# A fused mixer and feed-forward layer: retention's transposes two ticks sooner in the order, and softmax's scaling ahead of the next exponential

## The chip, the cores and the metric

The kernel runs on one core of a Trainium2 chip. The metric is device time in microseconds (us), the median over executions. The engines are TensorE (PE, with its weight loads PEld), VectorE (DVE), ScalarE (ACT), GpSimd (POOL) and SyncE (SP, here the queue that requests nearly all transfers). Each engine works through its own instructions in the order in which the program gives them.

## The reference, cut to what matters

One layer over 256 tokens of width 1024, all in fp32. The change touches the token mixer's two halves, attention and retention:

```python
proj = h @ w_in                                  # q, k, v of both, a gate rg, gates g_a and g_r
y_a  = moba_attention(mq, mk, mv)                # 8 heads of 64; one block of 256 keys, so plain causal softmax
y_r  = silu(rg) * head_norm(retention(rq, rk, rv))          # 4 heads, values of 256
merged = sigmoid(g_a) * (y_a @ w_proj_moba) + sigmoid(g_r) * (y_r @ w_proj_ret)
y = merged @ w_out
x = layer_norm(ALPHA * x + g1 * y, ...)          # then the feed-forward part and a second norm
```

## The kernel before, in words

All products of activations with weights are made in three matmuls of split operands: every fp32 weight half (128 x 1024) is split into a high part `whi` (an ACT copy with rounding, L1264) and a low part `wlo` (a DVE subtraction, L1278), and the product is high by high, high by low and low by high (`mm3`, L123 to L125). Activations are split in the same way by `split` (ACT L100, then DVE L101). A weight arrives as 1 MB in one of four buffers `raw`, requested on SP's queue (L110) when DVE has finished with the buffer's former content. Between the weight halves DVE also makes the products of the conditioning vector with its matrix (`ada`, L263, with its read of the sum; L989 ends a section); these use `raw` buffers too.

Nothing schedules at run time: the program writes the instructions of all engines in one order. The main loop goes over *steps*, one weight half of 1024 columns each. Three times a step it advances the *side* generators by one tick (`run_sides`): once ahead of the preparation of further weight halves, once behind it and ahead of the step's matmuls, and once behind the matmuls. `mixers` (attention) and `retention` are such generators, and a `yield` is a tick; so a count of empty `yield`s sets where a side's work stands among the weights' work. `put_off(n, fn)` does something n steps later.

Attention: `scores` and `maxima` (DVE L1059) come four and two heads at a time into the tiles `sm`, then for iteration i ACT takes the exponential of head i-1 with its sum (L1082), DVE the reciprocal of that sum (L1090), and ACT scales head i-3 (L1087); groups of heads are then transposed on PE (L1098) and copied back (L1100). `L504` evacuates the products of the rotated queries and keys.

Retention: its values lie in `yr`, the tiles A8a and A8b, one for each half of the tokens. At the end ACT scales them by the norm (L1180), DVE multiplies them with the gate (L1184), PE transposes them in 16 pieces into the four PSUM banks 4 to 7 (L1199), and `split` makes of these the two tiles `yr2` (AYa and AYb).

What follows one another on PE there: the gate products of `winGr` (evacuated by the sigmoid at L537), `wpm` (attention's projection, two groups of 24 matmuls), and `wpr` (retention's projection, two groups of 48, which read `yr2`). The banks of one group of 512 columns are those of the group two before: the first group of `wpr` writes the banks of the first group of `wpm`, which DVE empties by

```python
dve.tensor_tensor(v, bk[t], v, OP.mult)       # L544, in pm_done
```

Of the kernel before, what the change touches and what calls it, by code (L numbers as in the profile page):

```python
# [9 lines left out]
AF = mybir.ActivationFunctionType  # L10
# [3 lines left out]
HM, DM = 8, 64  # L14
# [54 lines left out]
def _body(nc, a, out, pe, act, dve, sp, cst, wts, big, tmp, ps, dram):  # L69
    f = lambda ap: ap.bitcast(F32)  # L70

    def bank(i):
        return ps.tile([128, 512], F32, tag=f"P{i}", name=f"P{i}")
# [10 lines left out]
    def slot(n, shape, dt=F32):  # L84
        if n in pairs:
            assert pairs[n].dtype == dt
            return pairs[n].rearrange("p e (k t) -> p e k t", k=shape[2])
        if n not in place:
            return big.tile(shape, dt, tag=f"A{n}", name=f"A{n}")
        pair, e = place[n]  # L90
        assert pairs[pair].dtype == dt
        v = pairs[pair][:, e, :math.prod(shape[1:])]
        return v.rearrange("p (a b) -> p a b", a=shape[1]) if len(shape) == 3 else v
# [5 lines left out]
    def split(hi, lo, src):  # L99
        act.activation(hi, src, AF.Copy)  # L100
        dve.tensor_tensor(lo, src, f(hi), OP.subtract)  # L101
# [927 lines left out]
    def mixers():  # L1029


        for _ in range(3 * SCORES_AT):
            yield
        v = S["v"]
        S["decay"] = [slot(n, [128, 2, 384]) for n in ("6a", "6b")]
        for i in range(2):
            nc.gpsimd.dma_start(S["decay"][i], a["decay"][i])
        st, pt = {}, {}
        blk = [slice(128 * qb, 128 + 256 * qb) for qb in range(2)]

        def scores(h):


            S["sc"] = [bank(b) for b in (4, 7, 5, 6)]
            x = S["rot"][h // 4]
            for qb, c in enumerate(blk):
                for i in range(2):
                    for e in range(4):
                        s = slice(32 * e, 32 * e + 32)
                        pe.matmul(S["sc"][e][:, c], x[s, i, qb * 128:(qb + 1) * 128], x[s, 2 + i, :128 + 128 * qb],  # L1050
                                  start=i == 0, stop=i == 1)

        def maxima(h):

            for e in range(2):
                sm = S["sms"][:, (h + e) % (TL + 2)]
                mx = tmp.tile([128, 8], F32, name="mx", bufs=TL + 2)
                for qb, c in enumerate(blk):
                    dve.tensor_tensor_reduce(out=sm[:, c], in0=S["sc"][h % 4 + e][:, c],  # L1059
                                             in1=consts["mask"][:, 128 - 128 * qb:],  # L1060
                                             scale=-0.125, scalar=3.0e38, op0=OP.add, op1=OP.min,
                                             accum_out=mx[:, 2 + qb:3 + qb])
                st[h + e] = sm, mx

        def attend(h, p):

            for w in range(2):
                pT = [pt.pop(h + 2 * w + e) for e in range(2)]
                for kb, (o, c) in enumerate(((slice(0, 256), slice(0, 256)), (slice(128, 256), slice(256, 384)))):
                    for e in range(2):  # L1070
                        u = h + 2 * w + e
                        pe.matmul(p[64 * e:64 * e + 64, 256 * w + o.start:256 * w + o.stop],
                                  v[:, kb, 64 * u:64 * u + 64], pT[e][:, c], start=kb == 0, stop=kb == 1)
            return lambda: split(S["yah"][:, h // 2:h // 2 + 2], S["yal"][:, h // 2:h // 2 + 2],
                                 p.rearrange("p (w t) -> p w t", w=2))

        for i in range(HM + 5):
            yield
            if 0 <= i - 1 < HM:
                sm, mx = st[i - 1]  # L1080
                for qb, c in enumerate(blk):
                    act.activation(sm[:, c], sm[:, c], AF.Exp, scale=-1.0, bias=mx[:, 2 + qb:3 + qb],  # L1082
                                   accum_out=mx[:, 4 + qb:5 + qb])
            if 0 <= i - 3 < HM:
                sm, rx = st[i - 3]
                for qb, c in enumerate(blk):
                    act.activation(sm[:, c], sm[:, c], AF.Copy, scale=rx[:, 6 + qb:7 + qb])  # L1087
            yield
            if 0 <= i - 1 < HM:
                dve.reciprocal(mx[:, 6:8], mx[:, 4:6])  # L1090
            if i == HM + 4:
                S["yah"], S["yal"] = [slot(n, [128, 4, 256], F32R) for n in ("5", "15")]
                done = [attend(4 * g, bank(5 + g)) for g in range(2)]
            for h in {6: (0, 1), 9: (2, 3, 4, 5), 11: (6, 7)}.get(i, ()):
                sm, mx = st.pop(h)
                p = bank((4, 7, 4, 7, 5, 6, 4, 7)[h])
                for b in range(3):
                    pe.transpose(p[:, b * 128:(b + 1) * 128], sm[:, b * 128:(b + 1) * 128], ident)  # L1098
                pT = sm if h > 1 else slot(("9a", "9b")[h], [128, 384])
                act.activation(pT, p[:, :384], AF.Copy)  # L1100
                pt[h] = pT
            if i == 0:
                S["sms"] = slot(11, [128, TL + 2, 384])
            if i in (0, 4):
                scores(i)
            if i in (0, 2, 4, 6):
                maxima(i)
            if i == RET_AT:
                sides.append(retention())
            yield  # L1110
        for fn in done:
            fn()

    def retention():
# [13 lines left out]
        for n in range(4):  # L1128
# [8 lines left out]
            if n == 1:  # L1137
                yr = [slot(n, [128, 1024]) for n in ("8a", "8b")]
                for g in range(HR):
                    d_ = ds_.pop(g)  # L1140
                    p = bank(VALUES[g])
                    c = slice(g * 256, (g + 1) * 256)
# [33 lines left out]
        for g in range(HR + 1):  # L1176
# [4 lines left out]
            if g < HR:  # L1181
                c = slice(g * 256, (g + 1) * 256)
# [7 lines left out]
        yrh, yrl = [[t[:, i] for t in S["yr2"]] for i in range(2)]  # L1190
        for _ in range(3):
            yield
        for _ in range(8):
            yield
        ps = [bank(4 + i) for i in range(4)]
        for i, p in enumerate(ps):
# [108 lines left out]
    prep_to(FIRST + 2)  # L1305
    evac_B()
    sides = [mixers()]

    def run_sides():
# [148 lines left out]
```

## Time and profile before

| | |
|---|---|
| median of 3 executions | 424.75 us (423.34 to 424.86) |
| the profiled execution | 423.23 us, its span 421.5 us |
| PE busy | 412.2 us |
| DVE busy | 370.3 us |
| ACT busy | 251.6 us |
| granted TensorE clock | 1.0 |
| read from memory | 104.28 MB, 250 GB/s over the span |

The span runs from the first to the last instruction; the rest of the execution's time, 1.7 us, lies around it. A row of the timeline gives the start in us, the duration in us, the engine and line, the operation, what it writes and reads, and in brackets how long the engine was idle before it and what released it. Instructions of one engine overlap a little, so what one costs in a row of its like is best read from start to start. SP's rows are requests, not transfers.

### The profile page before, as it was taken

The numbers are of one execution on the slowest core, as the hardware profiler recorded it, in microseconds if no ns is written. First come the engines' busy times: TensorE is split into PE (matmuls) and PEld (weight loads), VectorE is DVE, ScalarE is ACT, GpSimd is POOL, SyncE is SP. The second block draws the span as 40 slices with busy tenths as digits, with TensorE's granted clock in tenths as the row PEclk, the third lists the DMA queues.
The fourth block names the chain that finished last, engine by engine and source line by source line (L and its number), as shares of the span: only waits on it lengthen the run. The fifth ranks groups of instructions, "written<-read, shape, count | busy, mean of one in ns | idle before, by whom it ended". The sixth has DMA issues, their size and how long they took to land.

```text
span 421.5 us, 5942 instructions
## 1 busy us (share of the span) xinstructions
PE 412.2 (98%) x2156; PEld 347.0 (82%) x2156; DVE 370.3 (88%) x593; ACT 251.6 (60%) x442; POOL 14.0 (3%) x26
## 2 busy tenths in 40 slices
PE   7999999999999999979999999999999999999995
PEld 4888888888878888868888898888888888888884
DVE  6979798889997689799987889999999998789996
ACT  5666568687994885435553896373554555455700
POOL 0000010000000100000000000100000000003200
PEclk9999999999999999999999999999999999999999
DMA  8998999656574969978882073895867877550002
GB/s 298 405 409 342 412 402 417 253 201 211 198 282 149 341 227 370 332 275 317 338 303 101 0 301 111 306 383 200 303 242 251 308 282 268 192 200 2 0 2 100
DMA packets 18685, 105.73 MB, mean 251 GB/s; under 512 B 2272, under 2 KB 3680, under 8 KB 7904
## 3 DMA queue, kind: packets, MB, share of 16 engines
q1 hardware_dynamic: 17136, 99.84, 62.6%
q0 software_dynamic: 1376, 4.99, 3.3%
q10 hardware_dynamic: 144, 0.52, 0.5%
q8 instruction: 17, 0.28, 0.3%
q14 instruction: 12, 0.10, 0.1%
HBM read 104.28 MB, written 1.06 MB: 250 GB/s over the span
## 4 chain that ended last, share of the span: by engine, by line
PE 79%; DVE 10%; DMA 4%; ACT 4%; issue 2%; DVEq 0%; ACTq 0%
PE P L134 21%; PE P L337 13%; PE P L138 11%; PE P L123 9%; PE P L125 9%; PE P L124 9%; DVE wlo L1278 2%; DVE junk L263 2%; DMA raw<-in_wpr 2%; DMA raw<-in_wpm 2%; ACT AYa L1134 1%; ACT whi L1264 1%; DMA raw<-in_m 1%; PE P L721 1%; PE P L724 1%
## 5 line engine op out<-in xcount | busy, mean ns | idle before, releaser
L1278 DVE TENSOR_TENSOR wlo<-raw,whi 128x1024 fp32r<-128x1024 f32 x118 | 141.8, 1219 | 15.8 <-ACT whi L1264 15.6
L1264 ACT ACTIVATE whi<-raw 128x1024 fp32r<-128x1024 f32 x118 | 121.3, 1054 | 39.0 <-DMA raw<-in_wpr 15.6
L134 PE MATMUL P<-AYa,whi 128*128 128x512 f32 x160 | 46.3, 391 | 0.0
L134 PE MATMUL P<-AYb,whi 128*128 128x512 f32 x160 | 43.0, 390 | 0.0
L337 PE MATMUL P<-whi,AH 128*128 128x512 f32 x160 | 41.6, 390 | 0.5 <-DVE AH L303 0.5
L263 DVE CUSTOM_DVE_ANT_0 junk<-raw,srow 128x1024 bf16<-128x1024 f32 x32 | 39.0, 1217 | 0.0
L123 PE MATMUL P<-whi,AH 128*128 128x512 f32 x96 | 38.0, 396 | 0.0
L125 PE MATMUL P<-whi,AH 128*128 128x512 f32 x96 | 37.4, 390 | 0.0
L124 PE MATMUL P<-wlo,AH 128*128 128x512 f32 x96 | 37.4, 389 | 0.0
L337 PEld LDWEIGHTS P<-whi,AH 128*128 128x128 f32 x160 | 30.0, 188 | 7.5 <-ACT whi L320 1.3
L134 PEld LDWEIGHTS P<-AYb,whi 128*128 128x128 f32 x160 | 30.0, 188 | 6.6
L134 PEld LDWEIGHTS P<-AYa,whi 128*128 128x128 f32 x160 | 28.8, 189 | 4.7
L481 ACT ACTIVATE A<-P 128x256 f32<-128x256 f32 x40 | 15.1, 377 | 29.0 <-PE P L138 17.1
L134 PE MATMUL P<-AH,whi 128*128 128x512 f32 x128 | 31.6, 394 | 0.0
L320 ACT ACTIVATE whi<-raw 128x512 fp32r<-128x512 f32 (+1 forms) x26 | 20.8, 824 | 17.4 <-DMA raw<-in_b 16.2
L323 DVE TENSOR_TENSOR wlo<-raw,whi 128x512 fp32r<-128x512 f32 (+1 forms) x26 | 23.6, 935 | 6.1 <-ACT whi L320 5.6
L134 PEld LDWEIGHTS P<-AH,whi 128*128 128x128 f32 x128 | 23.3, 188 | 5.1 <-issue 0.3
L138 PE MATMUL P<-AYb,wlo 128*128 128x256 f32 x160 | 25.7, 283 | 0.0
L138 PE MATMUL P<-AYa,wlo 128*128 128x256 f32 x160 | 25.6, 283 | 0.0
L138 PEld LDWEIGHTS P<-AYa,wlo 128*128 128x128 f32 x160 | 23.3, 190 | 1.6
L337 PE MATMUL P<-wlo,AH 128*128 128x512 f32 x80 | 23.2, 389 | 0.0
L810 DVE SCALAR_TENSOR_TENSOR A<-A,tables 128x255 f32<-128x255 f32 (+1 forms) x44 | 21.3, 483 | 1.6
(310 smaller groups left out, 760.0 us busy)
## 6 DMA issues: line engine op xcount, KB each, us to landing
raw<-in_ada SPq DMA_DIRECT2D x16, 1024.0 KB, 4.8
raw<-in_wup SPq DMA_DIRECT2D x11, 1024.0 KB, 6.4
raw<-in_wgate SPq DMA_DIRECT2D x11, 1024.0 KB, 6.0
raw<-in_wdown SPq DMA_DIRECT2D x11, 1024.0 KB, 5.0
raw<-in_wrot SPq DMA_DIRECT2D x8, 1024.0 KB, 8.0
raw<-in_m SPq DMA_DIRECT2D x4, 1024.0 KB, 8.3
raw<-in_b SPq DMA_DIRECT2D x4, 1024.0 KB, 7.3
raw<-in_winGr SPq DMA_DIRECT2D x4, 1024.0 KB, 5.4
```

The lines of the kernel that those rows point to most:

```text
L123: pe.matmul(o, lh, rh, start=start, stop=False)
L124: pe.matmul(o, lh, rl, start=False, stop=False)
L125: pe.matmul(o, ll, rh, start=False, stop=stop)
L134: pe.matmul(banks()[half], t[0][:, k * 128:(k + 1) * 128], x2(k), start=k == 0, stop=half > 0 and k == 7)
L138: pe.matmul(banks()[half][:, :256], t[1][:, k * 128:(k + 1) * 128], x2(k)[:, 0], start=False, stop=half == 0 and k == 7)
L263: dve.tensor_tensor_reduce(out=nobody(j if own else None), in0=raw, in1=srow, scale=1.0, scalar=0.0, op0=OP.mult, op1=OP.add, accum_out=mo ...
L320: act.activation(hi[:, o], raw[:, o], AF.Copy)
L323: dve.tensor_tensor(lo[:, o], raw[:, o], f(hi[:, o]), OP.subtract)
L337: pe.matmul(pa[b0 + c // 512 * 2 + t], x[xi][:, j, t * 128:(t + 1) * 128], ws[k][:, c:c + 512], start=first and (xi, k) == (0, 0), stop=la ...
L810: dve.scalar_tensor_tensor(g[:, 2 - n:], x[:, :254 + n], w(n), g[:, 2 - n:], op0=OP.mult, op1=OP.add)
L1264: act.activation(hi, src, AF.Copy)
L1278: dve.tensor_tensor(lo, src, f(hi), OP.subtract)
```

## The change

Two places are written in another order; no instruction is added, removed or made larger.

```diff
         for i in range(HM + 5):
             yield
+            if 0 <= i - 3 < HM:
+                sm, mx = st[i - 3]
+                for qb, c in enumerate(blk):
+                    act.activation(sm[:, c], sm[:, c], AF.Copy, scale=mx[:, 6 + qb:7 + qb])
             if 0 <= i - 1 < HM:
                 sm, mx = st[i - 1]
                 for qb, c in enumerate(blk):
                     act.activation(sm[:, c], sm[:, c], AF.Exp, ...
-            if 0 <= i - 3 < HM:
-                ...
...
-        for _ in range(8):
+        for _ in range(6):
             yield
         ps = [bank(4 + i) for i in range(4)]
```

In `retention` two ticks are taken out ahead of the transposes, so they and their splits are written ahead of the preparation of weight halves in that step and of its matmuls.

On PE the 16 transposes (L1199) stood between the two halves of `wpm`'s first group; they now stand ahead of the whole group, right behind the last matmul of `winGr`. On ACT, around the sigmoids of `winGr` (L537), in the difference of the two orders:

```order
 L537 ACTIVATE A_1569<-P_1583 128x512
-L1264 ACTIVATE whi<-raw 128x1024
-L100 ACTIVATE AYa<-P_1683 128x4x128
-L100 ACTIVATE AYa<-P_1684 128x4x128
-L100 ACTIVATE AYb<-P_1685 128x4x128
-L100 ACTIVATE AYb<-P_1686 128x4x128
-L1264 ACTIVATE whi<-raw 128x1024 x10
+L100 ACTIVATE AYa<-P_1661 128x4x128
+L100 ACTIVATE AYa<-P_1662 128x4x128
+L100 ACTIVATE AYb<-P_1663 128x4x128
+L100 ACTIVATE AYb<-P_1664 128x4x128
+L1264 ACTIVATE whi<-raw 128x1024 x11
```

The four splits have moved past one weight half, the first of the second unit of `wpr`; all that follows on ACT keeps its order.

On DVE, from the end of a section of `ada` (L989) to the emptying of `wpm`'s banks (L544), before:

```order
L989 TENSOR_TENSOR mod<-mod,first 128x8
L1278 TENSOR_TENSOR wlo<-raw,whi 128x1024
L263 ISA junk,mod<-raw,srow 128x1024
L263 ISA mod 128x1
L101 TENSOR_TENSOR AYa<-P_1683,AYa 128x4x128
L101 TENSOR_TENSOR AYa<-P_1684,AYa 128x4x128
L101 TENSOR_TENSOR AYb<-P_1685,AYb 128x4x128
L101 TENSOR_TENSOR AYb<-P_1686,AYb 128x4x128
L1278 TENSOR_TENSOR wlo<-raw,whi 128x1024
L263 ISA junk,mod<-raw,srow 128x1024
L263 ISA mod 128x1
L544 TENSOR_TENSOR A_1414<-P_1669,A_1414 128x512
```

and the same place now:

```order
L989 TENSOR_TENSOR mod<-mod,first 128x8
L101 TENSOR_TENSOR AYa<-P_1661,AYa 128x4x128
L101 TENSOR_TENSOR AYa<-P_1662,AYa 128x4x128
L101 TENSOR_TENSOR AYb<-P_1663,AYb 128x4x128
L101 TENSOR_TENSOR AYb<-P_1664,AYb 128x4x128
L1278 TENSOR_TENSOR wlo<-raw,whi 128x1024
L263 ISA junk,mod<-raw,srow 128x1024
L263 ISA mod 128x1
L1278 TENSOR_TENSOR wlo<-raw,whi 128x1024
L263 ISA junk,mod<-raw,srow 128x1024
L263 ISA mod 128x1
L544 TENSOR_TENSOR A_1414<-P_1697,A_1414 128x512
```

The four low halves of the split have moved past one weight half (the second of the first unit of `wpr`) and one product of `ada`. The first L1278 there is the last reader of a `raw` buffer, so SP's next request of `wpr` waits for it, though SP's own order and POOL's stay as they are.

In the softmax, on ACT, one iteration (exponential L1082 before and L1086 now, scaling L1087 before and L1082 now, for the two blocks of queries; `mx` holds the maxima, sums and reciprocals):

```order
 L1264 ACTIVATE whi<-raw 128x1024 x2
-L1082 ACTIVATE A_838,mx<-A_838,mx 128x128
-L1082 ACTIVATE A_838,mx<-A_838,mx 128x256
-L1087 ACTIVATE A_838<-A_838,mx 128x128
-L1087 ACTIVATE A_838<-A_838,mx 128x256
+L1082 ACTIVATE A_838<-A_838,mx 128x128
+L1082 ACTIVATE A_838<-A_838,mx 128x256
+L1086 ACTIVATE A_838,mx<-A_838,mx 128x128
+L1086 ACTIVATE A_838,mx<-A_838,mx 128x256
 L504 ACTIVATE AR_585<-P_1125 128x256
```

The scaling of head i-3 now stands ahead of the exponential of head i-1 in each iteration. DVE's and PE's orders there are unchanged.

More of the change, by code (lines that the diff above doesn't have):

```diff
@@ L1083, in mixers @@
                                    accum_out=mx[:, 4 + qb:5 + qb])
-            if 0 <= i - 3 < HM:
-                sm, rx = st[i - 3]
-                for qb, c in enumerate(blk):
-                    act.activation(sm[:, c], sm[:, c], AF.Copy, scale=rx[:, 6 + qb:7 + qb])
             yield
```

## The prediction

> **What bounds the kernel now.** I read the page's busy shares first, then who waited for whom on TensorE (PE) and its weight loads (PEld), then the chain that ended last, then the order of time around the two places that the change touches.
>
> ```profile
> PE 412.2 (98%) x2156; PEld 347.0 (82%) x2156; DVE 370.3 (88%) x593; ACT 251.6 (60%) x442; POOL 14.0 (3%) x26
> ```
>
> PE is busy for 412.2 of 421.5 us, so an edit that leaves its work alone can win only what PE idles. The waits (total us, times, longest) say where that is:
>
> ```profile
> PE P L123 <- DVE A L544: 2.5, 1, 2.5
> ...
> PEld P L123 <- issue: 2.9, 1, 2.9
> ...
> PEld P L1098 <- ACT A L1087: 0.7, 2, 0.5
> ```
>
> The largest idle time is one event: the first matmul of `wpr` waits 2.5 us for VectorE's (DVE's) L544. The other is small: the transposes of the softmax rows (L1098) wait twice, 0.7 us in all, for ScalarE's (ACT's) scaling at L1087. The windows (us, then busy time of PE, PEld, DVE, ACT, POOL, then the granted clock, DMA share, GB/s) bound it:
>
> ```profile
> 158.00:184.00 26.00, 23.59 (x113) 19.44 (x111) 22.23 (x35) 13.42 (x22) 0.00 (x0) 1.00 0.83 320
> 186.00:411.00 225.00, 225.00 (x1170) 193.10 (x1169) 205.33 (x317) 121.50 (x188) 10.96 (x16) 1.00 0.58 214
> ```
>
> Between 158 and 184 PE loses 2.4 us; from 186 to 411 it loses nothing, so no transfer or engine is late there, and what PE gains before 186 it keeps unless the sooner start makes something late. The chain shows what the long wait consists of:
>
> ```profile
> 158.07 6.89 DMA raw<-in_wpm
> ...
> 169.61 7.30 DMA raw<-in_wpr
> ...
> 177.96 0.59 ACT AYa L100
> ...
> 182.10 1.22 DVE junk L263
> 183.33 0.61 DVE A L544
> 184.08 0.47 PE P L123
> ```
>
> A transfer of `wpr` releases ACT, ACT does retention's splits (L100), DVE does its halves of them and more, and only then L544, which empties the PSUM bank that PE wants. Retention's splits have nothing to do with that transfer; they merely stand behind it on ACT.
>
> **The change, part 1: transposes and splits two ticks sooner.** The rows in order of time, PE first, then ACT, DVE and SP's queue:
>
> ```profile
> 168.78 0.39 PE L123 MATMUL P<-whi,A 128*128 128x512 f32 x1
> ...
> 171.51 0.60 PE L1199 MATMUL P<-ident,A8a 128*128 128x128 f32 x4
> ...
> 173.17 0.48 PE L123 MATMUL P<-whi,A 128*128 128x512 f32 x1
> ...
> 181.20 0.39 PE L125 MATMUL P<-whi,A 128*128 128x512 f32 x1
> ...
> 195.08 0.39 PE L123 MATMUL P<-whi,AYa 128*128 128x512 f32 x1
> ```
>
> ```profile
> 166.35 0.49 ACT L1180 ACTIVATE A8b<-A8b,sdr 128x256 f32<-128x256 f32 x1
> ...
> 172.44 1.07 ACT L537 ACTIVATE A<-P 128x512 f32<-128x512 f32 x2
> 176.99 1.06 ACT L1264 ACTIVATE whi<-raw 128x1024 fp32r<-128x1024 f32 x1 [3.49 <-DMA raw<-in_wpr]
> ...
> 179.87 1.08 ACT L1264 ACTIVATE whi<-raw 128x1024 fp32r<-128x1024 f32 x1
> 183.83 2.01 ACT L1264 ACTIVATE whi<-raw 128x1024 fp32r<-128x1024 f32 x2 [2.88 <-DMA raw<-in_wpr]
> ```
>
> ```profile
> 174.10 1.22 DVE L1278 TENSOR_TENSOR wlo<-raw,whi 128x1024 fp32r<-128x1024 f32 x1
> ...
> 178.57 1.29 DVE L101 TENSOR_TENSOR AYa<-P,AYa 128x512 fp32r<-128x512 f32 x2 [2.11 <-ACT AYa L100]
> ...
> 180.97 1.22 DVE L1278 TENSOR_TENSOR wlo<-raw,whi 128x1024 fp32r<-128x1024 f32 x1
> ...
> 183.25 1.28 DVE L544 TENSOR_TENSOR A<-P,A 128x512 f32<-128x512 f32 x2
> ...
> 189.01 1.28 DVE L544 TENSOR_TENSOR A<-P,A 128x512 f32<-128x512 f32 x2
> ```
>
> ```profile
> 175.35 0.33 SPq L110 DMA_DIRECT2D raw<-in_wpr  x1
> ```
>
> PE: the 16 transposes take 171.51 to 173.17, 1.66 us. They now stand ahead of `wpm`'s first 12 matmuls (from 168.78, weight loaded at once before). Same work, so no cost, if their rows are ready: the last scaling (L1180) is done at 166.84, 1.7 us of slack.
> ACT: the four splits fall into the 3.49 us in which ACT waits for `wpr`. The two L537 start at 172.44; at 0.48 us an instruction (four L100 from 177.96 to 179.87) the first split starts at 173.40. They end by 175.3, before the transfer lands at 176.99, so the weight half behind them loses nothing.
> DVE: L101 follows its L100 by 0.61 (178.57 less 177.96), 174.01; DVE comes free for them at 174.10. Four take 2.40 (178.57 to 180.97), until 176.50. Then the displaced pair L1278 and L263 and the next such pair, 2.28 each (180.97 to 183.25), until 181.06; the second pair needs the half that lands at 176.99, is done at 178.05 and wanted at 178.78: 0.7 us of slack. L544 starts at 181.06 instead of 183.25, and PE 0.83 later as now (184.08 less 183.25), at 181.89 instead of 184.08: **2.19 us**. PE's last matmul ahead of it starts at 181.20; 12 such take 2.73 (168.78 to 171.51), 0.23 each, so the next could go at 181.43, and 0.46 of the stall stays, with L544 still in front.
> SP: its order stays, but the `wpr` request of 175.35 waits for the displaced L1278 and goes out 2.40 later, at 177.75. What it takes to land is bounded by 183.83 less 175.35 (8.48) above and, below, by the 4.7 of the row quoted further down; I take 8.48, the same transfer's own: 186.2, a loss of at most 2.4. Behind it stand two weight halves on ACT, and on DVE L1278, L263 and the second pair of L544 (189.01 now). With 1.1 for the half and 2.28 for the pair that pair starts at 189.6 to 190, and the bank is wanted when the second group of `wpr` starts, 11.0 after the first (195.08 less 184.08), at 192.9. So 2 to 3 us of cover; that is late next if the cover goes. The following request, 185.69 in the trace, moves forward with DVE. I take nothing for both.
>
> **The change, part 2: scale before exponential.**
>
> ```profile
> 105.25 0.19 ACT L1082 ACTIVATION_READ_ACCUMULATOR A<-A,mx 128x1 f32 x1
> ```
>
> ```profile
> 109.18 0.16 DVE L1090 RECIPROCAL mx<-mx 128x2 f32<-128x2 f32 x1
> ...
> 111.77 0.16 DVE L1090 RECIPROCAL mx<-mx 128x2 f32<-128x2 f32 x1
> ```
>
> ```profile
> 109.41 2.01 ACT L1264 ACTIVATE whi<-raw 128x1024 fp32r<-128x1024 f32 x2
> 112.16 0.40 ACT L1082 ACTIVATE A<-A,mx 128x128 f32<-128x128 f32 x1 [0.74 <-DVE mx L1059]
> ...
> 113.06 0.79 ACT L1087 ACTIVATE A<-A,mx 128x128 f32<-128x128 f32 x2
> ...
> 114.28 0.40 ACT L1082 ACTIVATE A<-A,mx 128x128 f32<-128x128 f32 x1
> ...
> 115.16 0.79 ACT L1087 ACTIVATE A<-A,mx 128x128 f32<-128x128 f32 x2
> ```
>
> ```profile
> 114.24 1.14 PE L1098 MATMUL P<-ident,A 128*128 128x128 f32 x9
> ...
> 116.19 0.48 PE L123 MATMUL P<-whi,AH 128*128 128x512 f32 x1
> ```
>
> At 111.42 ACT is free and waits 0.74 for the maxima of the newer head. The older head's scaling (two instructions, 0.69 to the next start) fits in there, since its reciprocal ran at 109.18. The exponential stays at 112.16; evacuation and the next scaling then fill the 1.22 between 113.06 and 114.28 in the other order (that head's reciprocal is of 111.77), and the next exponential stays at 114.28 too. So head 5's scaling ends near 114.4 instead of 115.95. PE's 12 transposes, 114.24 to 116.19, took 1.95; 16 took 1.66 in part 1, so 12 take 1.25. **0.70 us** between these, which is also the 0.7 of the wait. From below the wait on PE's own row, 0.2 at one place, would be the end; I take 0.70, since start to start is what the next matmul sees. ACT saves the same 0.7, as its idle time is filled. Exponentials of the earlier heads start up to 0.7 later; DVE's backlog hides that: head 4's sum was read at 105.44, and its reciprocal ran at 109.18.
>
> **Sum.** 2.19 + 0.70 = 2.89 us: 423.23, the profiled execution, becomes 420.34. The median before, 424.75, lies 1.52 above that execution; less 2.89 it is 421.86. I give the middle, **421.1**.
>
> **Rivals.**
> 1. *The first part alone pays.* From 139 on the chain runs over ACT and over two transfers (158.07 and 169.61). If these don't land sooner with their requests, L544 is where part 1 puts it and PE's 0.70 is spent waiting for it: 2.19 us, 421.04 on the profiled execution, 422.6 on the median. For it: DMA is 0.83 busy in 158 to 184. Against: the requests wait for DVE, not for the queue.
> 2. *More than the sum.* If the executions without a profile are 1.5 us slower because the `wpr` transfer of 169.61 lands later, it leaves the chain with the splits: the gain is 2.89 + 1.52 = 4.41, 420.34 on the median. Nothing in one trace shows it. Their stall would be 2.65 (184.08 less 181.43) + 1.52 = 4.2 us.
> 3. *Given back.* The later `wpr` request uses up its cover: landing 8.48 + 3 us after it, PE waits at the second group and the net gain is at most 1 us, 422.2 on the profiled execution. For it: transfers differ. Against: 2 us of cover beyond the slowest reading.
> 4. *Slower.* The transposes now head `wpm`'s 24 matmuls and wait for the last L1180, which stands behind a weight half that the second `wpm` transfer releases (158.07, 6.89). If that lands x later, PE stops for x - 1.7. The row of all requests (shortest, median, longest to landing) has
>
> ```profile
> DMA to landing us min/median/max: 4.7/5.7/9.9
> ```
>
> so 3 us more is possible: a stop of 1.3, still a gain. It decides from x = 4.6; at x = 6.9, a landing twice as long, PE stops 5.2 and the time is 423.23 - 2.89 + 5.2 = 425.5.
>
> [...] After the 2.65 us stop the row from 186 has a granted clock of 1.00, so a stop of that length costs only itself. [...]
>
> **How the numbers follow.** About 0.5%, 2.1 us, is what can be told from no change. The sum: 0.50. Rival 1: 0.25, on the edge of that bound, so 0.10 of it faster and 0.15 same. Rival 2: 0.10. Rival 3: 0.10. Rival 4: 0.05. Of the sum's 0.50 I put 0.05 on same, for scatter between executions. Faster 0.45 + 0.10 + 0.10 = 0.65, same 0.30, slower 0.05. The range: below, 420.34 less the 0.46 that stays of the stall and a little scatter, 419.6; above, the median less half the sum, 423.3, which takes in rivals 1 and 3 and leaves out rival 4 and the worst of 3.
>
> **What would show it.** Right: the L1199 transposes follow the last `winGr` matmul without a gap; ACT's four splits lie before its wait for `wpr`; the wait of PE on L544 is 0.3 to 0.6 us instead of 2.5; L1098's wait is gone; from the second `wpr` group to the tail PE has no new wait. Wrong: a wait of L1199 on L1180, of the second `wpr` group on L544 or on a transfer, or the same wait of 2.5 with another engine's name.

## The result, and the profile after

| | executions | median us | range |
|---|---|---|---|
| before | 6 | 424.81 | 423.34 to 425.33 |
| changed | 6 | 420.99 | 420.12 to 421.45 |

The ratio is 0.9916, with a 95% interval of 0.9895 to 0.9936: the changed kernel is faster by 3.8 us. The profiled execution took 420.91 us, with a span of 419.2 us; against the profiled execution before (423.23) that is 2.32 us. Two numbers for one change, 3.8 and 2.3, are what the experiments had to explain. (A few disturbed executions far above the others are left out of all comparisons and counts.)

The busy times have not moved; this is the page's row of the changed kernel:

```profile
PE 412.1 (98%) x2156; PEld 346.7 (83%) x2156; DVE 370.4 (88%) x593; ACT 251.7 (60%) x442; POOL 14.0 (3%) x26
```

The waits of PE and of PEld, in the same columns as before (total us, times, longest):

```profile
PE P L123 <- DVE A L544: 1.0, 1, 1.0
```

```profile
PEld P L123 <- issue: 1.4, 1, 1.4
```

The wait on L544 has fallen from 2.5 to 1.0, and L1098 is no longer in either list. The windows (busy time of PE, PEld, DVE, ACT, POOL, then granted clock, DMA share and GB/s):

```profile
158.00:184.00 26.00, 24.96 (x119) 20.61 (x118) 23.60 (x36) 12.55 (x20) 0.00 (x0) 1.00 0.91 326
186.00:409.00 223.00, 223.00 (x1164) 191.63 (x1163) 204.22 (x315) 121.89 (x189) 10.96 (x16) 1.00 0.57 212
```

PE now loses 1.04 us between 158 and 184, and still nothing behind. The chain of work that ended last, at this place (start, us, what):

```profile
163.53 6.95 DMA raw<-in_wpr
...
170.56 1.07 ACT whi L1264
...
171.65 1.23 DVE wlo L1278
...
174.23 1.20 DVE AYa L101 x2
175.42 1.20 DVE AYb L101 x2
...
180.03 1.14 DVE junk L263
...
181.18 0.61 DVE A L544
...
181.93 0.47 PE P L123
```

The second transfer of `wpr` and ACT's splits (L100) are gone from the chain. What releases PE is now the first transfer of `wpr`, then one cast on ACT, and behind it only work of DVE. In order of time, PE, ACT and SP's queue:

```profile
167.85 0.40 PE L125 MATMUL P<-whi,AH 128*128 128x512 f32 x1
168.08 0.60 PE L1199 MATMUL P<-ident,A8a 128*128 128x128 f32 x4
...
180.50 0.39 PE L125 MATMUL P<-whi,A 128*128 128x512 f32 x1
181.93 0.47 PE L123 MATMUL P<-whi,AYa 128*128 128x512 f32 x1 [1.04 <-DVE A L544]
```

```profile
170.56 2.01 ACT L1264 ACTIVATE whi<-raw 128x1024 fp32r<-128x1024 f32 x2 [3.53 <-DMA raw<-in_wpr]
...
173.43 1.09 ACT L100 ACTIVATE AYa<-P 128x512 fp32r<-128x512 f32 x2
...
176.76 2.01 ACT L1264 ACTIVATE whi<-raw 128x1024 fp32r<-128x1024 f32 x2 [1.27 <-DMA raw<-in_wpr]
184.15 2.01 ACT L1264 ACTIVATE whi<-raw 128x1024 fp32r<-128x1024 f32 x2 [5.38 <-DMA raw<-in_wpr]
```

```profile
163.53 0.33 SPq L110 DMA_DIRECT2D raw<-in_wpr  x1
...
177.81 0.33 SPq L110 DMA_DIRECT2D raw<-in_wpr  x1
```

The transposes follow `winGr`'s last matmul 0.23 later, without a gap. ACT's splits start at 173.43 and lie ahead of its wait for `wpr`. The first `wpr` matmul is at 181.93 instead of 184.08, 2.15 us sooner; but PE's last `wpm` matmul is at 180.50, so PE could have gone on at 180.73.

At the softmax, ACT and PE:

```profile
111.21 0.81 ACT L1082 ACTIVATE A<-A,mx 128x128 f32<-128x128 f32 x2
112.16 0.40 ACT L1086 ACTIVATE A<-A,mx 128x128 f32<-128x128 f32 x1
...
113.59 0.80 ACT L1082 ACTIVATE A<-A,mx 128x128 f32<-128x128 f32 x2
```

```profile
114.25 1.47 PE L1098 MATMUL P<-ident,A 128*128 128x128 f32 x12
115.47 0.48 PE L123 MATMUL P<-whi,AH 128*128 128x512 f32 x1
```

The scaling fills what was idle ahead of the exponential, which starts at 112.16 as before. The twelve transposes take 1.22 us (115.47 less 114.25) instead of 1.95.

### The profile page after: what moved, and what is told of

The parts are those of the page before. It is cut to its first block, busy times and chain, and to the rows that moved or that the text cites. A ratio compares the mean times of both kernels' runs of the same rounds, so it can differ in the third digit from the quotient of the medians.

```text
span 419.2 us, 5941 instructions
## 1 busy us (share of the span) xinstructions
PE 412.1 (98%) x2156; PEld 346.7 (83%) x2156; DVE 370.4 (88%) x593; ACT 251.7 (60%) x442; POOL 14.0 (3%) x26
## 4 chain that ended last, share of the span: by engine, by line
PE 88%; DVE 6%; ACT 3%; DMA 2%; issue 1%; DVEq 0%; ACTq 0%
PE P L134 25%; PE P L337 13%; PE P L138 13%; PE P L123 9%; PE P L125 9%; PE P L124 9%; DVE junk L263 2%; DMA raw<-in_wpr 2%; DVE wlo L1278 2%; ACT AYa L1134 1%; ACT whi L1264 1%; PE P L721 1%; PE P L723 1%; PE P L724 1%; PE P L1050 1%
## 5 line engine op out<-in xcount | busy, mean ns | idle before, releaser
L1278 DVE TENSOR_TENSOR wlo<-raw,whi 128x1024 fp32r<-128x1024 f32 x118 | 141.9, 1220 | 16.3 <-ACT whi L1264 16.2
L337 PE MATMUL P<-whi,AH 128*128 128x512 f32 x160 | 41.8, 391 | 0.1
L263 DVE CUSTOM_DVE_ANT_0 junk<-raw,srow 128x1024 bf16<-128x1024 f32 x32 | 39.0, 1220 | 0.0
L337 PEld LDWEIGHTS P<-whi,AH 128*128 128x128 f32 x160 | 29.7, 188 | 7.5 <-ACT whi L320 1.0
L337 PE MATMUL P<-wlo,AH 128*128 128x512 f32 x80 | 23.2, 390 | 0.0
```

The costliest lines, as they stand in the source:

```text
L263: dve.tensor_tensor_reduce(out=nobody(j if own else None), in0=raw, in1=srow, scale=1.0, scalar=0.0, op0=OP.mult, op1=OP.add, accum_out=mo ...
L337: pe.matmul(pa[b0 + c // 512 * 2 + t], x[xi][:, j, t * 128:(t + 1) * 128], ws[k][:, c:c + 512], start=first and (xi, k) == (0, 0), stop=la ...
```

## The experiments

The theory after this trace: part 1 pays its 2.19 us. Part 2 pays its 0.7 us too, but this trace spends it in the wait on L544, since the first `wpr` transfer, requested at 163.53 instead of 164.22, still reached ACT at 170.56. Before, SP's queue and ACT had

```profile
164.22 0.33 SPq L110 DMA_DIRECT2D raw<-in_wpr  x1
```

```profile
170.52 2.00 ACT L1264 ACTIVATE whi<-raw 128x1024 fp32r<-128x1024 f32 x2 [2.73 <-DMA raw<-in_wpr]
```

so 0.7 us were won on the request and none on the landing. What the medians have beyond the traces is somewhere else.

**The first part alone, the second part alone, and the kernel before again.** One group, on one chip; the kernel before had there a median of 423.34 (21 executions).

```diff
-        for _ in range(8):
+        for _ in range(6):
             yield
         ps = [bank(4 + i) for i in range(4)]
```

> Part 1 alone (ticks 6, softmax order as before). Theory: in the trace of the changed kernel L544 starts at 181.1 whether or not PE is 0.7 sooner, since the wpr transfer that ACT waits for lands at 170.5 in both; so this kernel is as fast as the changed one (within 0.3 us of it, 420.7 to 421.3), PE's wait on L544 is about 0.5 us instead of 1.0, and L1098's wait of 0.7 is back. Rival, the sum as predicted: 0.7 us slower than the changed kernel, 421.7.

Measured: 420.95 (420.68 to 421.16, 6 executions), ratio 0.9926, interval 0.9908 to 0.9944. PE at the place:

```profile
181.46 0.39 PE L125 MATMUL P<-whi,A 128*128 128x512 f32 x1
181.98 0.47 PE L123 MATMUL P<-whi,AYa 128*128 128x512 f32 x1
```

The first `wpr` matmul stands at 181.98, 0.05 from the whole change's 181.93, with 0.3 us of idle time in front. So of these two traces the first part holds the whole gain.

```diff
+            if 0 <= i - 3 < HM:
+                sm, mx = st[i - 3]
+                for qb, c in enumerate(blk):
+                    act.activation(sm[:, c], sm[:, c], AF.Copy, scale=mx[:, 6 + qb:7 + qb])
             if 0 <= i - 1 < HM:
                 ...
-            if 0 <= i - 3 < HM:
-                ...
```

> Part 2 alone (ticks 8, softmax order changed). Theory: L1098's wait goes, and PE gives the 0.7 us back at L544, whose start is set by a transfer: no change against before (424.8, within 0.4), PE's wait on L544 about 3.2 us instead of 2.5. Rival, the sum: 0.7 us faster than before.

Measured: 422.86 (421.60 to 426.63, 11 executions), ratio 0.9978, interval 0.9958 to 0.9997. Beside the same chip's 423.34 that is 0.5 less, between the theory's nothing and the rival's 0.7. The profiled execution was the longest of them, 426.63. PE's rows show why, then the windows:

```profile
180.90 0.39 PE L125 MATMUL P<-whi,A 128*128 128x512 f32 x1
184.83 0.77 PE L123 MATMUL P<-whi,AYa 128*128 128x512 f32 x1 [3.54 <-DVE A L544]
...
186.25 0.63 PE L123 MATMUL P<-whi,AYa 128*128 128x512 f32 x1
186.67 0.63 PE L124 MATMUL P<-wlo,AYa 128*128 128x512 f32 x1
```

```profile
184.00:185.00 1.00, 0.17 (x1) 0.20 (x2) 1.00 (x4) 0.21 (x1) 0.00 (x0) 0.52 0.02 8
...
190.00:191.00 1.00, 1.00 (x4) 0.74 (x3) 1.00 (x3) 0.00 (x0) 0.00 (x0) 0.57 1.23 344
```

PE's stop is longer here, 3.70 us from start to start (184.83 less 180.90 and 0.23). Against the first trace of the kernel before, the last `wpm` matmul is 0.30 sooner and the first `wpr` matmul 0.75 later, as ACT's cast at the second `wpr` landing is (177.74 for 176.99). From within the stop on the granted clock is half for 6.8 us (from about 184.04, as 0.52 of the first window means 0.96 us at half, to about 190.86; every window between has 0.50). The matmuls follow each other at 0.42 to 0.43 us instead of 0.23.

The kernel before, unaltered, with a profile:

> The kernel before, unchanged, for a second trace and the scatter. Theory of a longer stall (rival 2 of the prediction): an execution near 424.9 has a wait of about 4 us on L544, 1.5 more than the traced one at 423.2, and its wpr transfer lands later than 176.99. Rival: the 1.5 us lie elsewhere, and the wait on L544 is 2.5 us here too.

Measured: 423.22 (422.49 to 425.52, 12 executions), in two groups: nine up to 423.49 and three from 424.34. The profiled execution, 424.69, is of the upper group. PE and the windows:

```profile
181.60 0.39 PE L125 MATMUL P<-whi,A 128*128 128x512 f32 x1
184.12 0.47 PE L123 MATMUL P<-whi,AYa 128*128 128x512 f32 x1 [2.13 <-ACT whi L1264]
```

```profile
185.00:186.00 1.00, 1.00 (x5) 0.76 (x4) 1.00 (x2) 0.00 (x0) 0.00 (x0) 0.57 0.78 328
186.00:187.00 1.00, 1.00 (x4) 0.80 (x3) 1.00 (x3) 0.00 (x0) 0.00 (x0) 0.50 1.04 442
187.00:188.00 1.00, 1.00 (x3) 0.79 (x3) 1.00 (x2) 0.00 (x0) 0.00 (x0) 0.50 1.03 426
188.00:189.00 1.00, 1.00 (x5) 0.74 (x3) 1.00 (x1) 0.00 (x0) 0.00 (x0) 0.72 1.02 434
```

The stop is no longer than in the first trace of this kernel: 2.29 us (184.12 less 181.60 and 0.23), where that one had 2.65. (The row names ACT's cast, but the matmul stands 0.83 behind the start of L544, here at 183.29, as in the first trace: 184.08 less 183.25.) Yet here the clock is half behind it, for 3.4 us (0.86 us of the first of these windows, two whole ones, and 0.56 of the last), and eight matmuls lose 0.2 us each, 1.6 us. That is the difference between the two groups.

**Matmuls in the stop.** If the upper group is the clock's, it must vanish when PE has something to do. Nine matmuls are added to the kernel before where it waits; they write to a bank that nobody reads.

```diff
                 dve.tensor_tensor(v, bk[t], v, OP.mult)
+            if c == 1:
+                spare, y = bank(4), S["yah"]
+                for _ in range(9):
+                    pe.matmul(spare, y[:, 0, :128], y[:, 0:2].rearrange("p a b -> p (a b)"), start=True, stop=True)
```

> The kernel before, with 9 matmuls (128x512, 0.23 us each, 2.05 us) added on PE behind wpm's last one, into a bank that nobody reads: they fill PE's wait on L544 of 2.3 to 2.65 us and end before it does. Theory: the slower executions of before have the clock at half for 3.4 us behind that wait (8 matmuls at 0.43 instead of 0.23, 1.6 us, in the second trace of before); with PE kept busy the clock stays at 1.00 and the slower executions go: all between 422.5 and 423.6, a median some 0.5 us below before's, though work was added. Rival: the clock falls for another reason, or the added work costs its time: both groups stay, or 0 to 2 us more than before.

Measured: 423.27 (422.61 to 423.63, 12 executions), ratio 0.9984, interval 0.9966 to 1.0002. Beside it, on the same chip, the kernel before took 423.34 (422.12 to 427.28, 22 executions), with ten of them above the filled kernel's highest, eight of the ten at a lower mean clock (0.996 or less). PE, then the windows:

```profile
181.67 2.20 PE L548 MATMUL P<-A 128*128 128x512 f32 x9
184.41 0.47 PE L123 MATMUL P<-whi,AYa 128*128 128x512 f32 x1 [0.53 <-DVE A L544]
```

```profile
184.00:186.00 2.00, 1.59 (x7) 1.36 (x8) 2.00 (x4) 1.13 (x2) 0.00 (x0) 1.00 0.62 164
186.00:188.00 2.00, 2.00 (x11) 1.63 (x10) 2.00 (x3) 0.00 (x0) 0.00 (x0) 1.00 1.01 418
```

The first `wpr` matmul is no sooner than before (184.41), and the clock stays at 1.00. The upper group is gone: useless work bought the full clock. The expected 0.5 off the median did not come (423.27 against 423.34), since on this chip fewer than half of the executions before lie in the upper group. The mean granted clock that is recorded with each execution tells the same over four groups on four chips. Of the 86 executions of the kernel before in them,

| mean granted clock | executions | us | median |
|---|---|---|---|
| up to 0.996 | 33 | 424.30 to 427.28 | 424.84 |
| above 0.996 | 53 | 421.99 to 424.60 | 423.14 |

The 23 executions of the changed kernel in its first run and in the three repetitions below all lie above 0.996, at 419.66 to 421.67 with a median of 420.42. The filled kernel's twelve do so too. (Four of the 53 are above 423.7 at a full clock; no trace shows why.)

Among the executions above 0.996, each kernel against the kernel before on the same chip, the medians differ as follows: the first part alone gains 2.19 and 1.53 us (two chips), the second part alone 0.49, the whole change 2.85, 2.96 and 2.62 (three chips). With the clock out of the comparison the whole change gains what the sum of 2.89 said, to 0.3.

**The changed kernel again, and what holds L544.** The changed kernel ran once more as the reference of a second group.

> The changed kernel, unchanged, for a second trace and a comparison on one chip. Theory: PE resumes with wpr at 181.9 to 182.0 after a wait of 1.0 to 1.4 us and the clock stays at 1.00 behind it; times 420.1 to 421.5, about 2.3 us below the faster executions of before and 3.9 below the slower. Rival: the shorter wait brings the clock down too, in some executions: a second group near 422.5.

Measured: 420.34 (419.98 to 420.66, 6 executions), ratio 0.9914, interval 0.9886 to 0.9942. PE's wait on L544 is 0.2 us there, and the first `wpr` matmul at 181.40.

On DVE two products of `ada` (L263, 1.2 us each) stand between the retention's splits and L544. The next kernel is the changed one with the places of two sections of `ada` altered, so that none stands there; it ran in both groups.

```diff
-    for sec, at in ((2, (7, 8, 10, 12)), (3, (13, 14, 15, 17)), (4, (16, 18, 19, 20)), (5, (38, 41, 44, 47))):
+    for sec, at in ((2, (7, 8, 10, 12)), (3, (17, 20, 21, 22)), (4, (13, 14, 15, 16)), (5, (38, 41, 44, 47))):
```

> The changed kernel with the conditioning products (L263, and their transfers) of two sections placed otherwise: none between the first wpr unit and the emptying of wpm's banks; two units go behind the third wpr unit. Theory: what is left of PE's wait (1.0 us on its own row, 1.4 from the last matmul) is DVE's two L263 ahead of L544, 2.3 us, and the transfers they need; without them the wait is gone, 1.2 to 1.4 us faster than the changed kernel, 419.6 to 419.8. Rival: DVE, 90% busy behind that place, is late later with the two L263 it then has to do, and nothing is won or up to 1 us lost.

> The changed kernel with the conditioning products aside, again, beside the changed kernel on one chip. Theory: 1.2 us below the changed kernel from PE's first L337 to the first wpr matmul; in device time 0.5 to 1.2 below it, as the start of PE scatters by 1 us with the first transfers.

Measured: 420.49 (419.83 to 421.76, 6 executions) in the first group, and 420.71 (419.81 to 422.18, 7) in the second, beside the changed kernel's 420.34. The wait on L544 is gone in both traces. In the first of them no other wait of PE on DVE follows, but there PE's first L337 waits 1.1 us at the start of the kernel, which it doesn't in the first trace of the changed kernel, and the last `wpm` matmul stands at 181.49 instead of 180.50. In the second trace a new one does follow:

```profile
PE P L555 <- DVE A L564: 0.7, 1, 0.7
```

DVE owes the products anyway, and in this execution it is late at L564 instead. By the medians nothing is won in either group. The same kernel with the old order in the softmax:

> As f3, with the softmax order of before (exponential first). Theory: where PE has no wait on L544 left, L1098's wait of 0.7 us is on the path again, so this one is 0.7 us slower than f3. Rival: the softmax order is worth nothing in any setting: as f3.

Measured: 421.45 (420.51 to 422.17, 10 executions). That is 0.74 more than with the new order, by medians whose ranges overlap. Its trace has no wait on L564.

A smaller move, with sections 3 and 4 at (17, 19, 20, 21) and (13, 14, 15, 16), and once more the changed kernel beside it (what the text calls roundings of `ada` and of the gate are the products L263 and the low halves L101, and its first split of A is the emptying of the banks, L544):

> The changed kernel with the two late groups of VectorE's ada roundings (L263) moved by a single place each, so that none of them stands between the roundings of the gate (L101) and the first split of A (L544). Theory (the first split of A ends last before the first wpr matmul, and the L263 ahead of it on VectorE costs it about 1.3 us): TensorE has no wait on L544 over 0.3 us; the first wpr matmul comes 0.2 to 0.5 us behind the last wpm matmul; no wait on L564 as with the larger move, as VectorE is delayed elsewhere by one place only; the time is 0.3 to 1.0 us below the changed kernel's (419.5 to 420.3). Rival (VectorE owes the roundings anyway and is late at a later place): the wait on L544 goes, a wait of 0.5 us or more on a VectorE line takes its place behind it, and the time is within 0.3 us of the changed kernel's or above it.

> The changed kernel, unaltered, as the reference of the run beside it on the same chip. Both theories: 420.0 to 421.0 us, a wait of TensorE on L544 between 0 and 1.2 us in the traced execution, no fall of the granted clock behind it.

Measured: 421.88 (420.38 to 424.98, 12 executions), ratio 0.9973, interval 0.9950 to 0.9995; the changed kernel beside it 420.18 (419.66 to 421.67 in five), ratio 0.9922, interval 0.9898 to 0.9946. PE of the smaller move:

```profile
PE P L555 <- DVE A L564: 1.0, 2, 0.7
```

The rival again: L544 is on time, L564 is not, and the kernel is slower than the changed one. From the first `wpr` matmul (180.80) to the end its traced execution takes 238.5 us, 1.4 more than the changed kernel's beside it, and 1.0 of that is this wait. (Its two longest executions, 424.70 and 424.98, have a lower mean clock, 0.946 and 0.996; no trace shows where.) The trace of the changed kernel in this group was the telling one. ACT, then PE:

```profile
169.33 2.01 ACT L1264 ACTIVATE whi<-raw 128x1024 fp32r<-128x1024 f32 x2 [2.23 <-DMA raw<-in_wpr]
```

```profile
180.54 0.39 PE L125 MATMUL P<-whi,A 128*128 128x512 f32 x1
180.77 0.39 PE L123 MATMUL P<-whi,AYa 128*128 128x512 f32 x1
```

In this execution the transfer lands 1.23 us sooner than in the first trace of the same kernel, PE does not wait at all, and the first `wpr` matmul stands at 180.77. The theory that part 2's 0.7 us is always spent in the wait has fallen; it depends on the landing.

**The first part alone against the whole change.** Two groups on two chips can't settle 0.7 us, so both ran beside each other.

> The first part alone (transposes and splits two ticks sooner, the softmax in its old order), a second time, beside the whole change on the same chip. Theory A (L544 follows the landing of the first wpr transfer by a fixed 10.5 us; the 0.7 us of the softmax counts only in executions in which that transfer lands soon enough, before 169.4): the first wpr matmul is at 181.7 or later, since its last wpm matmul is; the median lies 0.2 to 0.7 us above the whole change's. Theory B (the softmax's 0.7 us is always spent in the wait on L544): the two medians agree within 0.2 us.

> The whole change, beside the first part alone on the same chip. Theory A: the first wpr matmul at the later of 11.4 us behind the first wpr cast on ScalarE and 0.23 us behind the last wpm matmul, thus anywhere from 180.7 to 182.0; median 0.2 to 0.7 us below the first part alone. Theory B: the medians agree within 0.2 us, and the first wpr matmul is where it is without the softmax's part.

Measured: 421.58 (420.85 to 422.24, 9 executions) for the first part alone, and 420.49 (419.96 to 421.21, 6) for the whole change; before, 424.04. PE of the first part alone, then of the whole change:

```profile
181.44 0.39 PE L125 MATMUL P<-whi,A 128*128 128x512 f32 x1
182.22 0.47 PE L123 MATMUL P<-whi,AYa 128*128 128x512 f32 x1 [0.39 <-DVE A L544]
```

```profile
180.59 0.39 PE L125 MATMUL P<-whi,A 128*128 128x512 f32 x1
180.83 0.47 PE L123 MATMUL P<-whi,AYa 128*128 128x512 f32 x1
```

The whole change is 1.09 us faster, more than the 0.2 to 0.7 expected, and the traces have its first `wpr` matmul 1.39 sooner. In both traces it stands 11.37 behind ACT's cast at the first `wpr` landing (see the table), and the cast is 1.40 sooner (169.46 for 170.86). Of that the request has 0.86 (163.61 for 164.47), close to the 0.85 by which the last `wpm` matmul is sooner (180.59 for 181.44); the other 0.54 is a shorter way from the request to ACT, which differs by more than that between executions of one kernel and is not shown to come from the softmax. By the medians the softmax's part does pay on top of the first.

All traces of the two orders together, in us:

| execution | cast at the first `wpr` landing | cast at the second | last `wpm` matmul | first `wpr` matmul | from there to the end of the span |
|---|---|---|---|---|---|
| before | 170.52 | 176.99 | 181.20 | 184.08 | 237.4 |
| before again | 171.10 | 177.03 | 181.60 | 184.12 | 238.9 |
| second part alone | 171.32 | 177.74 | 180.90 | 184.83 | 240.1 |
| before, filled | 170.34 | 177.32 | 181.45 | 184.41 | 237.2 |
| first part alone | 170.62 | 176.65 | 181.46 | 181.98 | 237.4 |
| first part alone, again | 170.86 | 176.12 | 181.44 | 182.22 | 237.5 |
| changed | 170.56 | 176.76 | 180.50 | 181.93 | 237.3 |
| changed, second | 170.03 | 176.37 | 180.84 | 181.40 | 237.2 |
| changed, third | 169.33 | 175.15 | 180.54 | 180.77 | 237.1 |
| changed, fourth | 169.46 | 175.35 | 180.59 | 180.83 | 237.4 |

Three things can be read from it. From the first `wpr` matmul on every execution takes 237.1 to 237.5 us, except the two with the clock at half, which take 1.6 and 2.8 more than the middle of these. And in the six with the first part, that matmul stands at the later of two times, within 0.02 us: 11.37 behind the cast, or 0.23 behind the last `wpm` matmul. In the four without it, the matmul hangs on the other transfer: it stands 7.09 behind the cast at the second `wpr` landing, in all four (184.08 less 176.99, for one), while from the first cast it is 13.02 to 14.07. So what the first part gains is the time between the two casts less 4.28 (11.37 less 7.09): 2.19 by the first trace of the kernel before, and 1.65 by the second.

## Why the prediction was right, and where it was not

The forecast of 421.1 us lies 0.1 from the median of 420.99, and 0.6 to 0.9 above the medians of the repetitions (420.34, 420.18, 420.49), all within the range. That it came so close is luck: it is the middle of two sums, 420.34 and 421.86, which differ by 1.52 us that the prediction did not explain, and the repetitions lie at the lower of the two.

**Part 1** came out as worked: with the landings of the first trace before, the matmul moves from 184.08 (7.09 behind the second cast) to 181.89 (11.37 behind the first), which is the 2.19, and the first trace of the changed kernel has L544 and the matmul at the instants that the sum gave, within 0.05. ACT's splits start at 173.43 (173.40 was said). The transposes find their rows ready; rival 4 did not occur. The later `wpr` request went out at 177.81 (177.75) and was on ACT at 184.15, 6.3 us after, not 8.5, so the cover held, and with it rival 3 fell.

**Part 2** was sized right on PE (0.73 for 0.70), but the *sum* was wrong in taking it as always additive. In the first trace the gain up to the first `wpr` matmul was 2.15, which is rival 1 to 0.04. In the other three it was 2.68, 3.31 and 3.25. The rival's condition, a landing that doesn't follow its request, differs from execution to execution: the request goes out at 163.5 to 163.9, and the cast follows it 5.8 to 7.0 us later. Where it lands soon, the 0.46 that was to stay of the stall goes as well, and 2.19 + 0.70 + 0.46 = 3.35 is the most there is. The 2.89 stands in the middle of what was seen. The wait on L544, said to be 0.3 to 0.6 us, was 1.0 and 0.2 in two of the traces and absent in the other two.

**The step that failed** is the one from the profiled execution to the median. The 1.52 us between them was carried along as a constant, which gave 421.86. It was the clock: 33 of the 86 executions before have a lower mean clock and are 1.7 us longer (424.84 less 423.14), and the median of the three that were shown, 424.75, lies at their times (no clock is on record with it). In the four traces of the change the stop is 1.20 us from start to start at most (181.93 less 180.50 and 0.23), and no execution of it shows the loss. So the 420.34 of the profiled execution held for the medians of the repetitions too, as rival 2 said, but not by its mechanism. ACT's cast at the second `wpr` landing, in the trace with the loss,

```profile
177.03 1.06 ACT L1264 ACTIVATE whi<-raw 128x1024 fp32r<-128x1024 f32 x1 [2.96 <-DMA raw<-in_wpr]
```

is where it was without it (176.99), and the stop is no longer. Over the executions with a full clock on all chips the gain is 2.7 (423.14 less 420.42), and that is the sum. The 3.8 us of the first comparison have more in them, since the median before, 424.81, lies 1.7 above the full clock's 423.14; that the changed kernel's 420.99 lies 0.6 above 420.42 takes some of it back.

**The clock.** The prediction said that a stop of 2.65 us costs only itself. One execution had shown that, and it does not hold in general: a stop of 2.29 cost 1.6 us more. In the trace with that loss PE resumes at 184.12, and the granted clock is half from about 185.14 to 188.56, 3.4 us. With the second part alone, where PE stops from 181.13 to 184.83, it is half from about 184.04, still inside the stop, to 190.86, 6.8 us. In the first trace of the kernel before, PE stops from 181.43 to 184.08, and every window of 1 us from 176 to 196 has 1.00. So the length of the stop alone does not tell: 2.29 and 3.70 us were followed by half clock, 2.65 was not. Why is not shown: no run sets a stop of a chosen length or place.

## What to carry to other kernels

Where PE stops for some 2 us in an otherwise full kernel, look at the granted clock behind the stop in more than one execution: two groups of times can be the clock's, as here (medians of 424.84 and 423.14). Here the change, which leaves a stop of 1.20 us at most in its four traces, and the filling, which leaves one of 0.53, both removed the upper group. Gains at two places of one chain add up only if what ends last at the second place moves as well; ask for each what releases it, and how much that scatters from one execution to the next. An engine that owes work (DVE with the `ada` products) need not be relieved by moving the work past one wait: in two of the four traces with the products moved it was late at the next, by 0.7 and 1.0 us.

## What the hardware showed that was not expected

- A stop of PE of 2.29 us was followed by 3.4 us at half clock, and one of 3.70 us came with 6.8 us of it; one of 2.65 us was followed by none, and no run shows why. With nine matmuls into a spare bank, which leave a stop of 0.53 us, all twelve executions had a mean clock above 0.996.
- The same transfer of 1024 KB, requested at nearly the same instant (163.53 and 163.57) in two executions of one kernel, was on ACT at 170.56 and at 169.33, in a stretch (158 to 184) where the DMA share was 0.91 in the first of the two. This scatter of 1.2 us is larger than the 0.7 us that the second part moves.
